# Two of the four channel groups of a causal depthwise convolution, moved from GpSimd and VectorE to TensorE as products with diagonal matrices

## Chip, cores and metric

One core of one Trainium2 chip runs the whole kernel in one launch. The metric is the device time in microseconds (us) of one execution. A measurement gives the median of several runs; a profile is one further execution, with its own time.

## The reference, cut to what matters

The kernel computes one decoder layer on 256 tokens of width 1024: a token mixer, cross-attention and a mixture of 32 experts. The mixer projects its input once and feeds three branches, a sparse attention (NSA), a convolution module and a gated linear attention (GLA), which are then merged. Only the convolution changes. It has 512 channels, 31 taps and is causal:

```python
a, gate = jnp.split(u_pair, 2, axis=-1)
u = a * jax.nn.sigmoid(gate)                      # (256 tokens, 512 channels)
y = conv(u, w, padding 30 on the left)            # y[t, c] = sum_k w[k, c] * u[t + k - 30, c], depthwise
y = y + b
out_b = silu(layer_norm(y, g, beta))              # over the 512 channels
```

## The kernel before, in words

**Layout.** Channels lie on the 128 partitions, in four groups m = 0 to 3 of 128 channels, and tokens along the free dimension. The tile `cu` (in the code `u`) holds the gated input with 30 zero columns in front, `cp` holds 34 numbers for each channel (31 taps, the bias, the norm's scale and shift), and `cy` (`y`) is the running sum.

**The taps.** `conv_out` (L305) returns the function `end`, which the layer calls at L601. It issues 31 taps for each of the four groups (L323 to L325). Groups 0, 1 and 2 go to VectorE (DVE): a `tensor_scalar` for tap 0 (L315), then 30 fused multiply-adds (L320). Group 3 goes to GpSimd (POOL), with two instructions for a tap: a product into one half of the tile `csg` (L317), then a sum (L318). So VectorE has 93 instructions and GpSimd 61.

**After the taps** come the layer norm over channels (L326 to L345), the gate (L346 to L348), and a split of the result into a high and a low part, `coh` and `col` (L349 to L351), which `merge` for branch 1 (L1611) multiplies by its weights.

**Splits.** Nearly every large product on TensorE is made from two fp32r halves of each operand. `wslot` (L121) gets 1 MB of weights by DMA; ScalarE (ACT) copies the high half `wh` (L80) and VectorE subtracts it to make the low half `wl` (L142, or L87 in four parts). Two such pairs are in flight. `project` (L145) then issues three matmuls for each block (L172). So every megabyte of weights passes through ACT and DVE before TensorE (PE) can use it.

**The order of the work.** A scheduler orders each engine's queue when the kernel is compiled: of what it takes to be ready it puts first what has the highest priority, and that is the order of the program, but for the blocks marked `high_priority`. At run time each engine works through its queue in that fixed order. `conv_out`'s `end` stands behind `gla` (L1596) and `nsa_in` (L1599) and ahead of `nsa` (L1607, which has high priority) and the three merges (L1610 to L1615). So taps fill places between the splits, the GLA and NSA inputs.

**GLA** (L426) is a chain over nine levels: differences and products on VectorE (L454 to L466), an exponential on ScalarE (L464), small matmuls on TensorE (L474 to L483) into banks of a pool of four PSUM banks (`bank`, L93), and copies on VectorE (L489 to L499). Then follow a norm with a power on GpSimd (L230), products (L518) and transposes (L91).

**After the front** (all up to about 430 us) the experts run: their weights, some 1 MB in each DMA, stream in on SyncE's queue while the matmuls of L1210 and L1255 use them.

Of the kernel before, what the change touches and what calls it, by code (L numbers as in the profile page):

```python
# [23 lines left out]
F32 = mybir.dt.float32  # L24
# [3 lines left out]
AF = mybir.ActivationFunctionType  # L28
ALU = mybir.AluOpType
# [5 lines left out]
P = 128  # L35
S = 256
# [5 lines left out]
TAPS = 31  # L42
# [28 lines left out]
class Front:  # L71
# [233 lines left out]
    def conv_out(self, pool):  # L305

        nc = self.nc
        u, cp = self.cu, self.cp
        y = pool.tile([P, 4, S], F32, name="cy")
        products = pool.tile([P, 4, S], F32, name="csg")  # L310
        def tap(m, k, v):
            scale, shift = cp[:, m, k:k + 1], cp[:, m, TAPS:TAPS + 1]
            eng = nc.gpsimd if m == 3 else nc.vector
            if k == 0:
                eng.tensor_scalar(y[:, m, :], u[:, m, 0:S], scale, shift, op0=ALU.mult, op1=ALU.add)  # L315
            elif m == 3:
                eng.tensor_scalar_mul(v, u[:, m, k:k + S], scale)  # L317
                eng.tensor_tensor(out=y[:, m, :], in0=y[:, m, :], in1=v, op=ALU.add)  # L318
            else:
                eng.scalar_tensor_tensor(y[:, m, :], u[:, m, k:k + S], scale, y[:, m, :], op0=ALU.mult, op1=ALU.add)  # L320

        def end():
            for k in range(TAPS):  # L323
                for m in range(4):
                    tap(m, k, products[:, k % 2, :])  # L325
            omean = pool.tile([P, P], F32, name="omean")  # L326
            nc.vector.memset(omean[:], 1.0 / 512)
            b = self.bank()
            for m in range(4):
                nc.tensor.matmul(b[:, 0:S], omean[:], y[:, m, :], start=(m == 0), stop=(m == 3))  # L330
            nc.vector.tensor_sub(y[:], y[:], b[:, None, 0:S].to_broadcast([P, 4, S]))
            sq = pool.tile([P, 4, S], F32, name="csg")
            nc.scalar.activation(sq[:], y[:], AF.Square)
            b = self.bank()
            for t in range(2):
                for m in range(4):
                    nc.tensor.matmul(b[:, t:t + 1], sq[:, m, t * P:t * P + P], omean[:, 0:1], start=(m == 0), stop=(m == 3))
            rs = pool.tile([P, 2], F32, name="crs")
            self.rpow(pool, rs[:], b[:, 0:2], 1e-5, 2)
            b = self.bank()  # L340
            for t in range(2):
                nc.tensor.matmul(b[:, t * P:t * P + P], rs[:, t:t + 1].to_broadcast([P, P]), self.ident[:], start=True, stop=True)
            nc.vector.tensor_mul(y[:], y[:], b[:, None, 0:S].to_broadcast([P, 4, S]))
            for m in range(4):
                nc.scalar.activation(y[:, m, :], y[:, m, :], AF.Identity, scale=cp[:, m, 32:33], bias=cp[:, m, 33:34])  # L345
            sg = pool.tile([P, 4, S], F32, name="csg")  # L346
            self.gate(sg[:], y[:])
            self.gated(y[:], sg[:], y[:])  # L348
            h = pool.tile([P, 4, S], F32R, name="coh", tag="cu")  # L349
            l = pool.tile([P, 4, S], F32R, name="col", tag="csg")  # L350
            self.split(h[:], l[:], y[:], 0.5)  # L351
            return h, l

        return end
# [1408 lines left out]
```

## Time and profile before

| what | value |
|---|---|
| median of 3 runs | 1439.58 us (1435.54 to 1441.28) |
| the profiled execution's own time | 1441.21 us |
| its span, first to last instruction | 1439.3 us |
| mean granted TensorE clock | 0.928 |
| busy over the span: PE / DVE / ACT / POOL | 85% / 42% / 24% / 9% |
| bytes moved by DMA | 472.24 MB, mean 328 GB/s |

Busy time is the time in which at least one instruction of the engine ran. Matmuls are pipelined, so a record's duration is longer than the distance to the next record; the distance between starts in an unbroken row of equal records is what one of them costs. PEld is the loading of the stationary operand, which runs beside the matmuls. An fp32 matmul shows as two records.

### The profile page before, as it was taken

The numbers are of one execution on the slowest core, as the hardware profiler recorded it, in microseconds if no ns is written. First come the engines' busy times: TensorE is split into PE (matmuls) and PEld (weight loads), VectorE is DVE, ScalarE is ACT, GpSimd is POOL, SyncE is SP. The second block draws the span as 40 slices with busy tenths as digits, with TensorE's granted clock in tenths as the row PEclk, the third lists the DMA queues.
The fourth block names the chain that finished last, engine by engine and source line by source line (L and its number), as shares of the span: only waits on it lengthen the run. The fifth ranks groups of instructions, "written<-read, shape, count | busy, mean of one in ns | idle before, by whom it ended". The sixth has DMA issues, their size and how long they took to land. (4 is left out here: it accounts for less than half of the span.)

```text
span 1439.3 us, 20736 instructions
## 1 busy us (share of the span) xinstructions
PE 1216.4 (85%) x8274; PEld 606.7 (42%) x8274; DVE 601.2 (42%) x1319; ACT 352.3 (24%) x711; POOL 136.6 (9%) x137
## 2 busy tenths in 40 slices
PE   8978999999999877886788978887987787898684
PEld 8767978989873211221222223122322121223121
DVE  5999876585643311332223223232332232323113
ACT  4424365444522110111111111121111021212100
POOL 3994000010011000030000000000000000000001
PEclk9989999999998987999999999899999998899888
DMA  9535816565878899999999879999999999869994
GB/s 305 174 74 125 241 60 189 180 212 179 312 286 314 357 415 415 414 416 416 417 414 415 346 299 413 415 370 413 416 415 413 415 416 416 351 273 414 416 416 177
DMA packets 110696, 472.24 MB, mean 328 GB/s; under 512 B 12081, under 2 KB 16276, under 8 KB 77756
## 3 DMA queue, kind: packets, MB, share of 16 engines
q1 hardware_dynamic: 108604, 464.63, 82.4%
q0 software_dynamic: 1648, 4.25, 1.3%
q8 instruction: 110, 1.80, 0.5%
q10 hardware_dynamic: 272, 1.05, 0.2%
q14 instruction: 62, 0.51, 0.1%
HBM read 468.58 MB, written 1.31 MB: 326 GB/s over the span
## 5 line engine op out<-in xcount | busy, mean ns | idle before, releaser
L1210 PE MATMUL g<-w,xT 128*32 128x512 f32 x1984 | 272.7, 659 | 84.7 <-DMA w<-in_expert_w_gu_dram 83.2
L1255 PE MATMUL m<-w,hT 128*32 128x512 f32 (+1 forms) x1440 | 206.0, 640 | 17.2 <-DMA w<-in_expert_w_down_dram 8.9
L1181 DVE TENSOR_SCALAR gc<-g 64x256 f32<-64x256 f32 (+1 forms) x70 | 29.2, 417 | 351.7 <-PE g L1210 251.1
L1210 PEld LDWEIGHTS g<-w,xT 128*32 128x32 f32 x1984 | 57.6, 114 | 270.5 <-DMA w<-in_expert_w_gu_dram 140.8
L142 DVE TENSOR_TENSOR wl<-w,wh 128x1024 fp32r<-128x1024 f32 (+1 forms) x96 | 114.9, 1233 | 65.8 <-ACT wh L80 65.6
L1182 ACT ACTIVATE row<-gc 64x256 f32<-64x256 f32 (+1 forms) x90 | 37.4, 417 | 383.5 <-DVE gc L1181 383.5
L80 ACT ACTIVATE wh<-w 128x1024 fp32r<-128x1024 f32 (+1 forms) x112 | 105.7, 990 | 102.0 <-PE big L172 66.6
L1229 DVE TENSOR_TENSOR ye<-ye,m 32x512 f32<-32x512 f32 x82 | 55.8, 681 | 143.6 <-ACT ye L80 142.4
L172 PE MATMUL big<-xh,wh 128*128 128x256 f32 x352 | 101.8, 289 | 0.0
L172 PE MATMUL big<-xl,wh 128*128 128x256 f32 x352 | 101.5, 288 | 0.0
L172 PE MATMUL big<-xh,wl 128*128 128x256 f32 x352 | 101.2, 288 | 0.0
L1255 PEld LDWEIGHTS m<-w,hT 128*32 128x32 f32 (+1 forms) x1440 | 47.1, 116 | 122.6 <-issue 95.1
L80 ACT ACTIVATE ye<-m 32x512 f32<-32x512 f32 (+1 forms) x83 | 48.8, 588 | 165.8 <-PE m L1255 164.8
L230 POOL TENSOR_TENSOR mv<-rp,nhalf 128x1 f32<-128x1 f32 x4 | 2.2, 554 | 893.6 <-DVE rp L229 800.9
L1210 PE MATMUL u<-w,xT 128*32 128x512 f32 x640 | 74.9, 609 | 0.0
L1266 PE MATMUL y<-ye,pgT 128*128 128x512 f32 x128 | 63.4, 641 | 9.8 <-issue 8.3
L172 PEld LDWEIGHTS big<-xl,wh 128*128 128x128 f32 x352 | 68.9, 196 | 1.1 <-issue 0.8
L172 PEld LDWEIGHTS big<-xh,wh 128*128 128x128 f32 x352 | 69.1, 196 | 0.2
L172 PEld LDWEIGHTS big<-xh,wl 128*128 128x128 f32 x352 | 68.5, 195 | 1.2 <-issue 1.1
L91 PE MATMUL m<-ident,uc 64*128 64x64 f32 (+1 forms) x168 | 29.1, 255 | 39.9 <-ACT hT L80 18.3
L1082 DVE TENSOR_SCALAR xT<-m,rowc 128x128 f32<-128x128 f32 x64 | 22.0, 405 | 84.4 <-PE m L91 73.4
L320 DVE SCALAR_TENSOR_TENSOR cy<-cu,cp,cy 128x256 f32<-128x256 f32 x90 | 48.2, 589 | 0.1
(431 smaller groups left out, 1767.5 us busy)
## 6 DMA issues: line engine op xcount, KB each, us to landing
w<-in_expert_w_gu_dram SPq DMA_DIRECT2D x256, 1024.0 KB
w<-in_expert_w_down_dram SPq DMA_DIRECT2D x127, 1024.0 KB
w<-in_w_in_dram SPq DMA_DIRECT2D x23, 1024.0 KB
w<-in_xa_wkv_dram SPq DMA_DIRECT2D x8, 1024.0 KB
w<-in_w_branch_dram SPq DMA_DIRECT2D x4, 1024.0 KB
w<-in_w_out_dram SPq DMA_DIRECT2D x4, 1024.0 KB
w<-in_xa_wq_dram SPq DMA_DIRECT2D x4, 1024.0 KB
w<-in_xa_wo_dram SPq DMA_DIRECT2D x4, 1024.0 KB
```

Of the source, the lines that this page charges most:

```text
L80: self.nc.scalar.activation(out, in_, AF.Copy, scale=scale)
L91: self.nc.tensor.transpose(out, in_, self.ident[0:k, 0:k])
L142: eng.tensor_tensor(out=l[:, js, :n], in0=t[:, js, :n], in1=h[:, js, :n].bitcast(F32), op=ALU.subtract)
L172: self.last = nc.tensor.matmul(dst, l, r, start=(b not in seen), stop=(last and i == 2), skip_group_check=True)
L320: eng.scalar_tensor_tensor(y[:, m, :], u[:, m, k:k + S], scale, y[:, m, :], op0=ALU.mult, op1=ALU.add)
L1082: self.nc.vector.tensor_scalar(out, in_, g, t, op0=ALU.mult, op1=ALU.add)
L1181: nc.vector.tensor_scalar_min(gc[0:n, s], g[:, s], 7.0)
L1182: nc.scalar.activation(sg[0:n, s], gc[0:n, s], AF.Sigmoid, scale=1.702)
L1210: nc.tensor.matmul(gu[32 * c:32 * c + 32, :], xT[:, k, :], W[k][:, c * 512:c * 512 + 512], start=(k == 0), stop=(k == 7), skip_group_check ...
L1229: nc.vector.tensor_add(ye[:, c, :], ye[:, c, :], pd[64 * c:64 * c + 32, :])
L1255: self.nc.tensor.matmul(pd[p0:p0 + w, :], hT[:, j, h * w:h * w + w], W[8 + k][:, c * 512:c * 512 + 512], start=(i < P // (2 * w)), stop=(i ...
L1266: self.nc.tensor.matmul(self.y[t][c][:], pgT[rows, t, :], ye[rows, v, :], start=False, stop=last, skip_group_check=True)
```

## The change

Groups 0 and 1 stay on VectorE as they were. Groups 2 and 3 become products on TensorE: for each tap k and group m ScalarE makes a 128x128 diagonal matrix whose diagonal holds the taps of the 128 channels (the identity times the column `cp[:, m, k]`), and TensorE multiplies it by the 256 shifted columns of `u` and adds into one half of a PSUM bank. These are plain fp32 products. The eight diagonals in flight lie in the space of `csg`. The bank, one of the pool of four, is held from the first product to the end. Two ScalarE instructions then copy its halves to `y` and add the bias. GpSimd does none of the convolution any more. No DMA is added, removed or moved.

```diff
         y = pool.tile([P, 4, S], F32, name="cy")
-        products = pool.tile([P, 4, S], F32, name="csg")
-        def tap(m, k, v):
+        diag = pool.tile([P, 4, S], F32, name="csg")[:].rearrange("p m (h c) -> p (m h) c", h=2)
+        mine = (2, 3)
+
+        def tap(m, k):
             scale, shift = cp[:, m, k:k + 1], cp[:, m, TAPS:TAPS + 1]
-            eng = nc.gpsimd if m == 3 else nc.vector
             if k == 0:
-                eng.tensor_scalar(y[:, m, :], u[:, m, 0:S], scale, shift, op0=ALU.mult, op1=ALU.add)
-            elif m == 3:
-                eng.tensor_scalar_mul(v, u[:, m, k:k + S], scale)
-                eng.tensor_tensor(out=y[:, m, :], in0=y[:, m, :], in1=v, op=ALU.add)
+                nc.vector.tensor_scalar(y[:, m, :], u[:, m, 0:S], scale, shift, op0=ALU.mult, op1=ALU.add)
             else:
-                eng.scalar_tensor_tensor(y[:, m, :], u[:, m, k:k + S], scale, y[:, m, :], op0=ALU.mult, op1=ALU.add)
+                nc.vector.scalar_tensor_tensor(y[:, m, :], u[:, m, k:k + S], scale, y[:, m, :], op0=ALU.mult, op1=ALU.add)
+
+        def product(bank, m, k, i):
+
+            d = diag[:, i % 8, :]
+            nc.scalar.activation(d, self.ident[:], AF.Identity, scale=cp[:, m, k:k + 1])
+            nc.tensor.matmul(bank, d, u[:, m, k:k + S], start=(i == 0), stop=(k == TAPS - 1), skip_group_check=True)

         def end():
+            b = self.bank()
             for k in range(TAPS):
                 for m in range(4):
-                    tap(m, k, products[:, k % 2, :])
+                    if m in mine:
+                        i = mine.index(m)
+                        product(b[:, i * S:i * S + S], m, k, k * len(mine) + i)
+                    else:
+                        tap(m, k)
+            for i, m in enumerate(mine):
+                nc.scalar.activation(y[:, m, :], b[:, i * S:i * S + S], AF.Identity, bias=cp[:, m, TAPS:TAPS + 1])
```

## Rows read from the trace of the kernel before

**Rows 1.** The page: the span, and from the part with 40 equal slices (36 us each) the busy tenths of PE and DVE, the granted TensorE clock in tenths, and the DMA rate in GB/s.

```profile
span 1439.3 us, 20736 instructions
...
PE   8978999999999877886788978887987787898684
...
DVE  5999876585643311332223223232332232323113
...
PEclk9989999999998987999999999899999998899888
...
GB/s 305 174 74 125 241 60 189 180 212 179 312 286 314 357 415 415 414 416 416 417 414 415 346 299 413 415 370 413 416 415 413 415 416 416 351 273 414 416 416 177
```

**Rows 2.** Busy time of each engine in three stretches (us from the span's start). Columns: length of the stretch; busy us and number of instructions of PE, PEld, DVE, ACT, POOL; granted clock; DMA share; GB/s.

```profile
36.00:152.00 116.00, 98.13 (x883) 88.69 (x883) 110.89 (x205) 44.26 (x77) 84.97 (x76) 0.93 0.51 127
152.00:420.00 268.00, 267.81 (x1812) 239.11 (x1811) 174.99 (x268) 128.44 (x248) 8.86 (x14) 1.00 0.60 203
420.00:1439.30 1019.30, 818.72 (x5352) 248.17 (x5351) 297.07 (x819) 162.77 (x363) 31.23 (x22) 0.91 0.95 385
```

**Rows 3.** TensorE's groups of matmuls by line and shape between 36 and 152 us. Columns: names, shapes, count | busy us, mean ns of one | idle us of the engine before them and what ended it. Of the first, second and fourth form there are three groups each, with the operands' halves exchanged (xl,wh and xh,wl; wh,xh and wh,xl), and of the L396 form too (xl,mh and xh,ml).

```profile
L172 PE MATMUL big<-xh,wh 128*128 128x256 f32 x118 | 35.0, 296 | 0.0
...
L172 PE MATMUL big<-wl,xh 128*128 128x512 f32 x32 | 13.6, 424 | 4.8 <-DVE wl L142 4.8
...
L483 PE MATMUL s<-gx 64*64 64x64 f32 x192 | 6.6, 231 | 6.5 <-DVE gad L495 5.4 <-DVE gx L466 1.1
...
L172 PE MATMUL big<-wl,xh 128*128 128x256 f32 x16 | 4.6, 289 | 0.2 <-DVE wl L142 0.2
...
L508 PE MATMUL s<-gv,gat 128*128 128x128 f32 x16 | 3.5, 346 | 0.0
...
L396 PE MATMUL s<-xh,mh 128*56 128x256 f32 x8 | 2.3, 282 | 0.0
...
L91 PE MATMUL s<-ident,goc 128*128 128x128 f32 x8 | 1.8, 288 | 3.1 <-DVE goc L518 3.1
...
L477 PE MATMUL s<-gx 64*64 64x64 f32 x16 | 0.9, 222 | 2.6 <-DVE gx L466 2.6
```

**Rows 4.** The timeline of TensorE (start us, duration us, instruction): the first and the last of 17 consecutive 256-column records, and the first and the last of 12 consecutive 512-column records.

```profile
102.00 0.28 PE L172 MATMUL big<-xl,wh 128*128 128x256 f32 x1
...
103.92 0.28 PE L172 MATMUL big<-xh,wl 128*128 128x256 f32 x1
...
53.35 0.39 PE L172 MATMUL big<-wl,xh 128*128 128x512 f32 x1
...
55.85 0.39 PE L172 MATMUL big<-wh,xh 128*128 128x512 f32 x1
```

**Rows 5.** Busy time in ten microseconds of the later front (columns as in Rows 2).

```profile
300.00:310.00 10.00, 10.00 (x46) 8.29 (x45) 7.28 (x11) 3.01 (x4) 1.00 (x1) 1.00 0.61 208
```

**Rows 6.** VectorE: the page's group of the taps (count | busy us, mean ns); then the taps and the weight split between 36 and 107 us (same columns); then the line views of the taps and of the split over the whole run (ns min/median/max, first and last start us).

```profile
L320 DVE SCALAR_TENSOR_TENSOR cy<-cu,cp,cy 128x256 f32<-128x256 f32 x90 | 48.2, 589 | 0.1
...
L320 DVE SCALAR_TENSOR_TENSOR cy<-cu,cp,cy 128x256 f32<-128x256 f32 x34 | 21.2, 678 | 0.0
...
L142 DVE TENSOR_TENSOR wl<-w,wh 128x1024 fp32r<-128x1024 f32 x11 | 15.0, 1399 | 0.0
...
L320 DVE SCALAR_TENSOR_TENSOR cy<-cu,cp,cy x90: 462/481/2547, 43.2 to 161.6; 128x256 f32<-128x256 f32 x90
...
L142 DVE TENSOR_TENSOR wl<-w,wh x96: 693/1221/1761, 16.0 to 405.7; 128x1024 fp32r<-128x1024 f32 x94, 128x512 fp32r<-128x512 f32 x2
```

**Rows 7.** GpSimd's two groups of conv instructions between 36 and 107 us (count | busy us, mean ns | idle before).

```profile
L317 POOL TENSOR_SCALAR csg<-cu,cp 128x256 f32<-128x256 f32 x30 | 42.5, 1427 | 16.9 <-DVE cp L288 16.8
...
L318 POOL TENSOR_TENSOR cy<-cy,csg 128x256 f32<-128x256 f32 x30 | 26.9, 896 | 1.3
```

**Rows 8.** The line views of two products of fp32 by fp32, 128x128 by 128x256 (two records each; of the first also its weight loads; ns min/median/max, first and last start us).

```profile
L763 PEld LDWEIGHTS s<-xkT,xq x32: 186/190/192, 359.3 to 366.1; 128*128 128x128 f32 x32
...
L763 PE MATMUL s<-xkT,xq x32: 377/379/483, 359.4 to 366.3; 128*128 128x256 f32 x32
...
L330 PE MATMUL s<-cy,omean x8: 379/379/483, 161.3 to 163.0; 128*128 128x256 f32 x8
```

**Rows 9.** ScalarE between 0 and 440 us: a 128x128 activation with a per-partition operand, and a copy of 128x256 out of PSUM (count | busy us, mean ns | idle before).

```profile
L615 ACT ACTIVATE ns<-ns,nmx 128x128 f32<-128x128 f32 x16 | 6.2, 393 | 3.3 <-DVE nmx L610 3.3
...
L80 ACT ACTIVATE gax<-s 128x256 f32<-128x256 f32 x2 | 0.7, 382 | 6.0 <-PE s L474 6.0
```

**Rows 10.** Busy time in four stretches of 4 us (columns as in Rows 2).

```profile
76.00:80.00 4.00, 4.00 (x16) 3.15 (x16) 4.00 (x8) 0.00 (x0) 3.92 (x5) 0.81 0.49 131
88.00:92.00 4.00, 3.89 (x29) 3.77 (x30) 4.00 (x7) 0.00 (x0) 3.92 (x4) 0.50 0.35 57
92.00:96.00 4.00, 4.00 (x36) 3.80 (x35) 4.00 (x8) 0.00 (x0) 3.92 (x5) 0.68 0.59 171
112.00:116.00 4.00, 4.00 (x26) 3.69 (x25) 3.88 (x11) 1.28 (x6) 0.00 (x0) 0.62 0.59 225
```

**Rows 11.** The tile col, the conv branch's result: when it is made and when TensorE first loads its weights with coh and col (ns min/median/max, first and last start us).

```profile
L85 DVE SCALAR_TENSOR_TENSOR col<-cy,coh x1: 1217/1217/1217, 210.1 to 210.1; 128x1024 fp32r<-128x1024 f32 x1
...
L172 PEld LDWEIGHTS big<-col,wh x32: 187/188/192, 228.5 to 253.2; 128*128 128x128 f32 x32
```

**Rows 12.** The waits between 36 and 152 us (us in total, times, longest us).

```profile
ACT gd L464 <- DVE gd L463: 12.2, 5, 4.2
```

## The prediction

> **What bounds the kernel now.** I read the page's slices first, then busy time by stage, then each engine inside the stage that the change touches.
>
> The slices show two regimes [rows 1]. From about slice 13 the DMA rate stands near 415 GB/s: the experts are paced by their weights, a fixed number of bytes (DMA share 0.95 from 420 us on [rows 2]). What the front loses or gains therefore reaches the end one for one, unless something re-orders the experts, which nothing here does. So the question is how long the front takes.
>
> The front has two parts [rows 2]. From 36 to 152 us VectorE is busy 110.9 of 116 us, TensorE 98.1, GpSimd 85.0, ScalarE 44.3. From 152 to 420 us TensorE is busy 267.8 of 268 us. There its records stand shoulder to shoulder: 46 in ten microseconds are 0.217 us each [rows 5], and an unbroken row of 512-column records runs at (55.85 - 53.35)/11 = 0.227 us [rows 4]. So TensorE sets the pace from 152 us on, and VectorE before that. All the convolution's taps lie in or close to the first part, the last one at 161.6 us [rows 6]. The branch's result `col` is there at 210.1 us and first used at 228.5 us [rows 11]: the convolution itself has 18 us to spare. The change matters only through what it does to the queues of others.
>
> How much of the 116 us does TensorE need? The 256-column records number 3x118 + 3x16 + 3x8 = 426 [rows 3] at (103.92 - 102.00)/16 = 0.120 us [rows 4], 51.1 us. The 512-column ones are 96 at 0.227, 21.8 us. The other 361 records are short; the four groups of them shown (232 records, 12.8 us busy [rows 3]) give 20 us for all in proportion, too much, since the busy time of a burst holds its tail. The weight loads, 88.7 us [rows 2], leave 15.8 for them. So TensorE needs 89 to 93 us and has 23 to 27 us of slack; I take 27, nearer to the loads because of the tails.
>
> That slack divides so. Waits for VectorE's low halves: 4.8 + 0.2 = 5.0 us; for the GLA copies `gad`, 5.4; for `gx`, 1.1 + 2.6 = 3.7; for `goc`, 3.1 [rows 3]. Time lost to the granted clock, busy time times what is missing from 1.00 (below 1 the stretch was partly at 1.2 GHz instead of 2.4): 4.00x0.19 + 3.89x0.50 + 4.00x0.32 + 4.00x0.38 = 5.5 us [rows 10], all right behind such waits. That leaves 4.3 us in small pieces.
>
> **What the change takes away.** VectorE loses 31 of its 93 tap instructions. 90 took 48.2 us [rows 6], 0.536 each, so 16.6 us. GpSimd loses all 61, 42.5 + 26.9 us and one more [rows 7]. While GpSimd worked, the taps took 678 ns on average against a median of 481, and the split 1399 against 1221 [rows 6]. If the remaining two thirds of the 34 taps fall to the median, 23x0.197 = 4.5 us return, and from 11 splits 2.0 us. VectorE would then stand at 110.9 - 16.6 - 6.5 = 88 of 116 us: no longer the bound.
>
> **What it adds.** 62 fp32 products of 128x128 by 128x256. The kernel has the same form elsewhere: 32 records over 359.4 to 366.3 us are 0.2226 each [rows 8], two for a product, 0.445 us. So 62x0.445 = **27.6 us of TensorE**. The other row of the form, 8 records in 161.3 to 163.0, gives 0.486 and 30.1 us as the upper end; its times are rounded over a seventh of the length, so I take the first.
>
> ScalarE makes 62 diagonals. No row has this exact instruction; a 128x128 activation with a per-partition operand took 393 ns, a whole 128x256 copy out of PSUM 382 [rows 9]. So 24.4 us for the diagonals and 0.8 for the two copies at the end, on an engine with 71.7 us free in the stretch. I cost them at nothing: idle ScalarE hides them. If that cover fails, a diagonal ahead of a weight copy makes it late by 0.4 us, and the low half and the three matmuls behind it too. The reverse wait is the risk: with eight diagonals in flight (3.6 us of products), TensorE stands when ScalarE is held longer. The PSUM bank held throughout leaves three for GLA. Fewer banks can't speed anything; the worst is some of the GLA waits above again. I take nothing, and leave it to the third case. No DMA is added or moved; what SyncE and GpSimd issue stays in its queue, and GpSimd's comes free earlier.
>
> **The sum.** How much of the 27 us do the lighter VectorE and the products between them fill? The waits for low halves and `gad` (10.4 us) are VectorE's backlog: I take 8.4 back. The slow clock followed these holes: 5.0 of 5.5. The `gx` and `goc` waits (6.8) are a chain through three engines in which products can stand, if the compiled order puts them there: half, 3.4. Of the small pieces half, 2.1. Together 18.9 us. These four shares are my estimates; the ends are 7 (only part of the backlog) and 27. So the front grows by 27.6 - 18.9 = **8.7 us**. Against the profiled execution's own 1441.2 us that is 1449.9; that execution stood 1.6 above the median of the runs, so against 1439.6 it is **1448 us**. The reasoning in a line: VectorE's backlog costs TensorE less than the work handed to it.
>
> Which measure of TensorE's room counts is the point on which a rule of the skill bears: busy matmul time leaves 116 - 98.1 = 17.9 us, the count of records 23 to 27 [rows 2, 4]. The Trainium skill (Perfetto Trace Analysis, Identifying the Most-Contended Engine) says that matmul busy time is no good measure of headroom, that the busy share of weight loading is better, and that the engine with the highest occupancy should be relieved first. By busy matmul time the change would cost at least 27.6 - 17.9 = 9.7 us; by the rule VectorE is the engine to relieve and the change should not hurt. The trace agrees with the rule on the measure from 36 to 152 us, and not after it, where weight loading is 8.29 of 10 us and the records leave no room [rows 5].
>
> **Rivals.**
>
> *Every hole is filled (not slower).* VectorE at 88 of 116 us is late for nothing, the products stand in every hole of GLA, and TensorE runs at full clock from 36 to 152 us. Then all 27 us come back: 27.6 - 27 = +0.6, 1440 us. If TensorE were held by its weight loads alone, a product would cost two loads of 190 ns [rows 8], 62x0.38 = 23.6, and the time would be 27 - 23.6 = 3.4 below, 1436 us. For it: the need for the products and the slack are of one size. Against it: TensorE's queue is fixed, and a chain of three engines keeps holes. It decides once less than about 6 us of holes are left.
>
> *Coupled queues (much slower).* A product waits for its diagonal, a diagonal for the product eight before it, and both stand in queues with the splits and GLA. ScalarE already stood 12.2 us in five waits for VectorE's `gd`, the longest 4.2 us [rows 12], longer than eight products last. If TensorE inherits these, only about 7 us come back: 27.6 - 7 = +20.6, 1460 us. Against it: the lighter VectorE shortens just these waits.
>
> *The products don't go into the holes.* They stand behind GLA and NSA inputs in priority, and share a pool of banks with them. If they come in one block after about 147 us, where TensorE is full, only the backlog and the clock come back, 13.4 us: +14.2, 1454 us. Against it: taps in the same place of the program began at 43.2 us [rows 6].
>
> **How the numbers follow.** A measurement of this kernel tells about 0.5%, 7.2 us, from no change: the lines are 1432.4 and 1446.8 us. The forecast, +4 to +13 us, has 0.56, of which 0.37 is above the upper line and 0.19 within. Every hole filled has 0.22: 0.17 within, and 0.05 faster, for what a re-ordered front may gain besides. Coupled queues have 0.15 and one block 0.07, both slower. So slower 0.59, same 0.36, faster 0.05. The range 1437 to 1460 reaches into the filled case and to the middle of the coupled one, and leaves out some 0.15; it holds the upper price of a product (+2.5 us).
>
> **What the changed profile should show.** No taps on GpSimd, 60 on VectorE with a mean near 490 ns. 124 product records at about 0.222 us apart where they are unbroken. VectorE between 36 and 152 us near 75% busy. The granted clock near 1.00 through the holes of before. Waits of TensorE for low halves and `gad` under 3 us. The stretch that did the work of 36 to 152 us longer by about 9 us, and the same work after it unchanged. `col` before it is needed. I am wrong if TensorE's stretch is not longer (all filled), if TensorE waits for diagonals by more than 5 us (coupled), or if the front's growth does not reach the end of the run.

## The result, and the profile after

The changed kernel takes **1455.55 us** (median of 6 runs, 1453.01 to 1458.59) against 1440.95 (6 runs) before: a ratio of 1.0092, 95% interval 1.0071 to 1.0113, or +13.3 us (the two medians differ by 14.6). The prediction was 1448 in 1437 to 1460, slower at 0.59. The profiled execution after took 1456.01 us, span 1454.2. Of one kernel below, the one with only VectorE's group as products, two of six runs (1474.29 and 1476.88 us) were in a slower state of the chip and are left out.

First the same three stretches as in [rows 2].

```profile
36.00:152.00 116.00, 109.43 (x951) 99.15 (x950) 88.81 (x192) 63.58 (x129) 15.83 (x15) 0.99 0.57 156
152.00:420.00 268.00, 266.43 (x1790) 239.08 (x1789) 161.81 (x238) 130.08 (x254) 8.68 (x12) 0.97 0.50 169
420.00:1454.00 1034.00, 831.83 (x5442) 265.88 (x5440) 305.58 (x833) 167.46 (x369) 31.83 (x23) 0.92 0.95 385
```

VectorE (the third busy time) fell from 110.9 to 88.8 us and the clock of the first stretch rose from 0.93 to 0.99: the relief is real. But the second stretch, at 1.00 before, is now at 0.97.

VectorE between 36 and 107 us, answering to [rows 6] (count | busy us, mean ns):

```profile
L318 DVE SCALAR_TENSOR_TENSOR cy<-cu,cp,cy 128x256 f32<-128x256 f32 x44 | 18.5, 480 | 0.0
L142 DVE TENSOR_TENSOR wl<-w,wh 128x1024 fp32r<-128x1024 f32 x12 | 16.4, 1400 | 0.0
L87 DVE TENSOR_TENSOR wl<-w,wh 128x512 fp32r<-128x512 f32 x8 | 5.0, 690 | 0.0
```

The small split before, in the same view:

```profile
L87 DVE TENSOR_TENSOR wl<-w,wh 128x512 fp32r<-128x512 f32 x8 | 7.0, 934 | 0.0
```

The taps dropped from 678 to 480 ns; the small split L87 from 934 to 690. The large split did not (1399 before; the reason is in the last section).

TensorE's groups between 36 and 165 us, with the idle time before them, answering to [rows 3]:

```profile
L324 PE MATMUL s<-cu,csg 128*128 128x256 f32 x124 | 27.0, 379 | 0.0
L172 PE MATMUL big<-wl,xh 128*128 128x512 f32 x32 | 12.5, 390 | 0.0
...
L494 PE MATMUL s<-gx 64*64 64x64 f32 x192 | 5.9, 224 | 1.2 <-DVE gad L506 0.8 <-DVE gx L477 0.4
...
L91 PE MATMUL s<-ident,goc 128*128 128x128 f32 x8 | 2.1, 338 | 4.0 <-DVE goc L529 4.0
...
L488 PE MATMUL s<-gx 64*64 64x64 f32 x16 | 0.9, 222 | 1.1 <-DVE gx L477 1.1
```

The waits for low halves are gone (5.0 before) and that for `gad` is 0.8 (5.4 before). The wait for `goc` is still there, at 4.0: no product stands in it. Where the products stand is in the tile view of the diagonals (first and last start at the end of the times) and in the timeline of TensorE (start, duration):

```profile
L324 PE MATMUL s<-cu,csg x124: 377/379/484, 131.7 to 158.4; 128*128 128x256 f32 x124
L323 ACT ACTIVATE csg<-ident,cp x62: 387/401/404, 38.4 to 155.3; 128x128 f32<-128x128 f32 x62
```
```profile
131.37 0.39 PE L589 MATMUL s<-cw,cmy 64*15 64x64 f32 x4
131.69 1.56 PE L324 MATMUL s<-cu,csg 128*128 128x256 f32 x6
...
157.28 1.46 PE L324 MATMUL s<-cu,csg 128*128 128x256 f32 x6
158.57 0.38 PE L341 MATMUL s<-cy,omean 128*128 128x256 f32 x1
```

All 124 records stand in **one block of 27 us**, right behind the last matmul of the NSA inputs (L589) and right ahead of the convolution's own mean (L341). While it runs VectorE waits 28.4 us for that mean. Behind it TensorE is slow. The 16 us from 160 to 176 before, then the same stretch after, then the wait in the latter:

```profile
160.00:176.00 16.00, 16.00 (x135) 15.51 (x134) 10.92 (x18) 5.07 (x5) 0.71 (x1) 1.00 0.64 227
```
```profile
160.00:176.00 16.00, 14.61 (x92) 13.99 (x91) 8.84 (x18) 6.63 (x20) 1.64 (x1) 0.68 0.18 67
```
```profile
166.78 0.80 PE L353 MATMUL s<-ident,crs 128*128 128x128 f32 x2 [1.39 <-POOL crs L230]
```

The convolution's norm is a chain from engine to engine with short matmuls, and after the block less other work stands beside it: in these 16 us 92 matmuls for 135, and between the mean (L341) and the chain's matmuls with `crs` (L353) 25 records of L172 where before there were 53. TensorE is idle for 1.4 us, and the granted clock goes from 1.00 to 0.68, partly at 1.2 GHz instead of 2.4. It is 1.00 up to 165.4 us, where the wait begins, and 0.53 in the wait and 0.50 in the 5.2 us behind it. So 1.4 + 14.6 x 0.32 = 6.1 us are lost here, an estimate that takes the clock's whole loss as time.

Milestones, taken in every kernel from the line views of three tiles: the last matmuls of the NSA inputs, the first product of `xkT` with `xq`, and the first expert matmul (start, us).

```
                 NSA inputs end   first xq   first expert   span
before               148.3          359.4        435.5      1439.3
after                131.1          378.9        454.6      1454.2
```

The work up to the NSA inputs ends 17.2 us earlier, the block puts 27 on top (its end, 158.6, is 9.7 after the 148.9 of before), and by the first expert matmul the delay is 19.1 us, so another 9.4 came behind the block. Not all of that is loss. The windows up to the end of the NSA inputs (before, then after), and one later stretch after:

```profile
0.00:148.85 148.85, 126.75 (x1088) 116.23 (x1088) 126.14 (x227) 59.10 (x99) 96.51 (x102) 0.93 0.59 170
```
```profile
0.00:131.55 131.55, 119.91 (x1076) 111.63 (x1076) 105.35 (x216) 61.31 (x107) 27.21 (x41) 0.96 0.64 190
220.00:260.00 40.00, 39.95 (x304) 37.38 (x304) 23.18 (x28) 18.59 (x31) 2.79 (x6) 0.96 0.67 198
```

TensorE did 1088 matmuls up to there before and 1076 after: 12 records of L172, at 0.12 us 1.4 us, only moved behind this milestone. With the 6.1 us of the norm's chain and 0.04 x 40 = 1.6 us of clock between 220 and 260 us that is 9.1 of the 9.4. `col` is made at 201.5 us and first used at 249.9: it is not late.

### The profile page after: what moved, and what is told of

It is laid out like the page before. It is cut to its first block, busy times and chain, and to the rows that moved or that the text cites. A ratio compares the mean times of both kernels' runs of the same rounds, so it can differ in the third digit from the quotient of the medians.

```text
span 1454.2 us, 20956 instructions
## 1 busy us (share of the span) xinstructions
PE 1238.6 (85%) x8398; PEld 634.5 (44%) x8398; DVE 573.1 (39%) x1288; ACT 377.0 (26%) x775; POOL 67.7 (5%) x76
## 5 line engine op out<-in xcount | busy, mean ns | idle before, releaser
L1266 PE MATMUL m<-w,hT 128*32 128x512 f32 (+1 forms) x1440 | 202.7, 635 | 18.6 <-DMA w<-in_expert_w_down_dram 10.3
L172 PE MATMUL big<-xh,wh 128*128 128x256 f32 x352 | 103.6, 294 | 0.0
L172 PE MATMUL big<-xl,wh 128*128 128x256 f32 x352 | 103.0, 293 | 0.0
L172 PE MATMUL big<-xh,wl 128*128 128x256 f32 x352 | 102.7, 293 | 0.0
L80 ACT ACTIVATE ye<-m 32x512 f32<-32x512 f32 (+1 forms) x83 | 48.8, 588 | 158.6 <-PE m L1266 157.6
L172 PEld LDWEIGHTS big<-xl,wh 128*128 128x128 f32 x352 | 70.4, 200 | 1.7 <-issue 1.6
L172 PEld LDWEIGHTS big<-xh,wh 128*128 128x128 f32 x352 | 70.6, 201 | 0.3
L172 PEld LDWEIGHTS big<-xh,wl 128*128 128x128 f32 x352 | 70.1, 200 | 1.3 <-issue 1.1
L91 PEld LDWEIGHTS m<-ident,uc 64*128 64x128 f32 (+1 forms) x168 | 17.4, 144 | 70.1 <-ACT hT L80 29.9
L1277 PEld LDWEIGHTS y<-ye,pgT 128*128 128x128 f32 x128 | 24.4, 200 | 46.7 <-issue 46.4
```

Of the source, the lines that this page charges most:

```text
L80: self.nc.scalar.activation(out, in_, AF.Copy, scale=scale)
L91: self.nc.tensor.transpose(out, in_, self.ident[0:k, 0:k])
L172: self.last = nc.tensor.matmul(dst, l, r, start=(b not in seen), stop=(last and i == 2), skip_group_check=True)
L1266: self.nc.tensor.matmul(pd[p0:p0 + w, :], hT[:, j, h * w:h * w + w], W[8 + k][:, c * 512:c * 512 + 512], start=(i < P // (2 * w)), stop=(i ...
L1277: self.nc.tensor.matmul(self.y[t][c][:], pgT[rows, t, :], ye[rows, v, :], start=False, stop=last, skip_group_check=True)
```

## Experiments

Theory A: the place in the program decides; the products, written behind GLA and the NSA inputs, come out as a block and leave the holes unused. Rivals: the shared pool of banks holds them back; the diagonals on ScalarE do; or the kernel simply has no room for 27.6 us. Ratios are to the kernel before on the same chip (its medians there: 1440.73 for the first four kernels below, 1441.24 for the next four, 1441.99 for the last three).

**A bank of its own for the products**

```diff
-            b = self.bank()
+        acc = self.ps_c.tile([P, 512], F32, name="cacc")
...
-        f.ps_s = front.enter_context(tc.tile_pool(name="ps_s", bufs=4, space=PSUM, side="right"))
+        f.ps_s = front.enter_context(tc.tile_pool(name="ps_s", bufs=3, space=PSUM, side="right"))
+        f.ps_c = front.enter_context(tc.tile_pool(name="ps_c", bufs=1, space=PSUM, side="right"))
```

> The products' PSUM bank comes from a pool of its own (one bank; the shared pool keeps three) and is asked for ahead of GLA. Theory A, the place in the program decides (lowest priority of what waits for TensorE until the NSA inputs are done): most of the 62 products still run in one block of about 24 to 27 us right behind the NSA inputs, 1453 to 1458 us. Theory B, the products only waited for one of the four banks that GLA and the NSA inputs keep taking: they begin near 40 us, stand in the holes, and the time is 1440 to 1447 us.

1454.07 us, 1.0088 [1.0059, 1.0117]. The products still form a block, 4.6 us earlier:

```profile
L324 PE MATMUL cacc<-cu,csg x124: 376/379/484, 127.1 to 154.6; 128*128 128x256 f32 x124
```

The first of them now stand ahead of the last matmul of the NSA inputs (131.3 us), but none near 40 us. The bank theory falls.

**No products, no diagonals** (the relief alone)

```diff
-                    if m in mine:
-                        i = mine.index(m)
-                        product(b[:, i * S:i * S + S], m, k, k * len(mine) + i)
-                    else:
+                    if m not in mine:
                         tap(m, k)
...
-                nc.scalar.activation(y[:, m, :], b[:, i * S:i * S + S], AF.Identity, bias=cp[:, m, TAPS:TAPS + 1])
+                nc.scalar.activation(y[:, m, :], u[:, m, 0:S], AF.Identity, bias=cp[:, m, TAPS:TAPS + 1])
```

> The products and their diagonals are left out (groups 2 and 3 get only the first shifted columns plus bias), so VectorE and GpSimd are relieved and TensorE and ScalarE get nothing. If the relief is worth what the trace of the changed kernel shows at the end of the NSA inputs (131.2 against 148.3 us): 1420 to 1424 us without any further gain, down to 1415 if the slow stretch behind the block of products goes too. Rival, TensorE's later work sets the front's end whatever happens before 150 us: 1437 to 1441 us.

1434.99 us, 0.9965 [0.9949, 0.9981]. The total lies between the two expectations. The front is the theory's: the first expert matmul comes at 420.5 us, 15.0 before that of before. The rest went in the experts, which took 1013.1 us from there on, against 1003.8 before. The clock is 1.00 where the norm's chain runs, so the relief alone does not slow it. Since two channel groups are not the convolution's here, tokens go to other experts; a later experiment checks this.

**The identity in place of the diagonals**

```diff
-            d = diag[:, i % 8, :]
-            nc.scalar.activation(d, self.ident[:], AF.Identity, scale=cp[:, m, k:k + 1])
-            nc.tensor.matmul(bank, d, u[:, m, k:k + S], start=(i == 0), stop=(k == TAPS - 1), skip_group_check=True)
+            nc.tensor.matmul(bank, self.ident[:], u[:, m, k:k + S], start=(i == 0), stop=(k == TAPS - 1), skip_group_check=True)
```

> The 62 products stay, but all take the identity as their stationary operand and ScalarE makes no diagonals (the sums of groups 2 and 3 are then unweighted). Theory A, part of the loss is that the 54 diagonals of the block (23.3 us of ScalarE) hold back the weight copies, so that TensorE is short of work and slow behind the block from 164 to 176 us: the copies are made during the block, 1446 to 1450 us. Rival, the block itself costs everything: 1454 to 1457 us.

1482.53 us, 1.0301 [1.0269, 1.0333]. The front is that of the change to within 0.3 us (first xq 379.1, first expert matmul 454.9), block included:

```profile
L322 PE MATMUL s<-cu,ident x124: 376/379/483, 131.9 to 158.5; 128*128 128x256 f32 x124
```

So the diagonals cost the front nothing, and do not place the block. The longer total lies behind 454.9 us: the overflow group of the experts (tile `xTo`) has 256 records against 192, so it too has other tokens.

**The products spread ahead of GLA's levels** (bank asked for ahead of GLA)

```diff
+        acc = self.bank()
+        def feed():
+            for k in range(TAPS):
+                for i, m in enumerate(mine):
+                    product(acc[:, i * S:i * S + S], m, k, k * len(mine) + i)
+                    yield
+        self.feed = feed()
...
+            for _ in range(7):
+                next(self.feed, None)
```

> As the changed kernel, but seven products stand ahead of each of GLA's nine levels in the program, and the bank is asked for ahead of GLA. Theory A, the order cost the difference to the forecast: the products fill GLA's waits, the block behind the NSA inputs and the slow stretch behind it are gone, 1440 to 1448 us. Rival, coupled queues: TensorE waits for diagonals and ScalarE for products inside GLA, 1453 to 1465 us.

1444.86 us, 1.0019 [0.9998, 1.0041]; first expert matmul 441.6, 13.0 before that of the change. The products' records (tile view), and the two stretches:

```profile
L324 PE MATMUL s<-cu,csg x124: 376/379/484, 74.0 to 109.4; 128*128 128x256 f32 x124
```
```profile
36.00:152.00 116.00, 114.06 (x970) 101.65 (x969) 84.18 (x192) 66.32 (x139) 14.30 (x14) 1.00 0.48 129
152.00:420.00 268.00, 267.82 (x1822) 238.27 (x1822) 165.19 (x242) 128.12 (x245) 8.28 (x13) 1.00 0.58 198
```

TensorE's idle time in the first stretch is 1.9 us (6.6 in the change) and the clock is 1.00 in both: the holes are filled and the norm's chain has cover again (more other matmuls beside it). By the two ratios order alone is worth 0.0073, about 10 us of the 13.3. It does not turn the change into a gain.

**The block alone, on the kernel before** (62 products with the identity, their sum times zero added; no relief)

```diff
+            spare = self.bank()
+            for k in range(TAPS):
+                for i in range(2):
+                    nc.tensor.matmul(spare[:, i * S:i * S + S], self.ident[:], u[:, 2 + i, k:k + S], start=(k + i == 0), stop=(k == TAPS - 1), skip_group_check=True)
+            for i in range(2):
+                nc.vector.scalar_tensor_tensor(y[:, i, :], spare[:, i * S:i * S + S], 0.0, y[:, i, :], op0=ALU.mult, op1=ALU.add)
```

> The kernel before with 62 fp32 products of the identity added behind its taps (no diagonals, nothing taken from VectorE or GpSimd; the sum is added times zero), so TensorE gets the block and nobody is relieved. Theory A (a block of products costs its full 27 us in a place where TensorE is full, and the experts pass it on one for one): the first expert matmul comes 25 to 30 us later than before's 435.5, and the time is 1465 to 1471 us. Rival (the experts give back part of what the front loses, as 19.1 us of delay at the first expert matmul became 14.9 at the end of the changed kernel): the front is later by as much, and the time is 1458 to 1464 us.

1472.11 us, 1.0229 [1.0191, 1.0266]. The tile views of the products and of the experts' tokens `xT`:

```profile
L329 PE MATMUL s<-cu,ident x124: 377/379/483, 148.6 to 175.3; 128*128 128x256 f32 x124
```
```profile
L1216 PE MATMUL g<-w,xT x1984: 589/592/1062, 463.5 to 1402.6; 128*32 128x512 f32 x199
```

The first expert matmul is 28.0 us later, for 27.6 forecast as the price of the products; the span grows by 27.2, the median by 30.9, 1.1 us more than theory A's upper end. What the front loses does reach the end. Behind this block the norm's chain is not slow: the clock of the second stretch is 1.00 and the wait for `crs` 0.35 us, with 33 records of L172 between mean and `crs`.

```profile
152.00:420.00 268.00, 267.50 (x1820) 239.82 (x1819) 163.30 (x248) 122.89 (x238) 7.77 (x12) 1.00 0.52 174
```
```profile
184.51 0.49 PE L348 MATMUL s<-ident,crs 128*128 128x128 f32 x2 [0.35 <-POOL crs L230]
```

So neither the block alone nor the relief alone slows the chain; in the change, which has both, it is slow. Why it has only 25 records there stays open.

**The data of "no products" on the kernel before**

```diff
+            for m in (2, 3):
+                nc.scalar.activation(y[:, m, :], u[:, m, 0:S], AF.Identity, bias=cp[:, m, TAPS:TAPS + 1])
```

> The kernel before with all its taps, but groups 2 and 3 are then overwritten by what the kernel without products puts there, so that the experts get the same tokens as in that run. It is the base for the relief alone. Theory A (the relief is worth at the end what it is worth at the first expert matmul, 15 us, and the other tokens made that run's experts longer): 1446 to 1451 us. Rival (the experts give the front's 15 us back): 1439 to 1442 us, 5 us above the run without products.

1472.47 us, 1.0224 [1.0188, 1.026]. As a base for times it failed: the overwriting copies stand in ScalarE's queue until GpSimd's last tap, 28.5 us, TensorE waits 25.3 us for GLA's `gad` behind them, and the front ends 21.3 us late. What it does show: its expert part takes 1014.0 us, as in the kernel without products (1013.1). The other tokens explain the longer experts there.

**Only GpSimd's group as products** (VectorE keeps three groups, four products ahead of each level; the edit is against the spread kernel)

```diff
-        mine = (2, 3)
+        mine = (3,)
-            for _ in range(7):
+            for _ in range(4):
```

> Only GpSimd's group becomes 31 products, four ahead of each of GLA's levels; VectorE keeps three groups of taps. Theory A (GpSimd's work mattered because VectorE's instructions are longer beside it): VectorE gets some 6 us back in the splits and taps, the products cost 13.8 us of which GLA's waits hide about half: 1438 to 1444 us. Rival (VectorE's own taps are what holds TensorE): the relief is small and the time is 1446 to 1452 us.

**1435.47 us, 0.9962 [0.9945, 0.9978]**: faster than both kernels. The first stretch, and VectorE between 36 and 107 us:

```profile
36.00:152.00 116.00, 111.63 (x983) 99.37 (x982) 105.48 (x227) 57.30 (x110) 18.03 (x16) 1.00 0.53 154
```
```profile
L318 DVE SCALAR_TENSOR_TENSOR cy<-cu,cp,cy 128x256 f32<-128x256 f32 x56 | 23.6, 478 | 0.0
L142 DVE TENSOR_TENSOR wl<-w,wh 128x1024 fp32r<-128x1024 f32 x10 | 11.8, 1218 | 0.0
```

First xq comes at 355.8 us, 3.6 before that of before, but the first expert matmul at 435.2, only 0.3 before. Between them stands a wait of TensorE on its own sequencer, ahead of the first expert matmul (the first line is before, the second this kernel; us, times, longest):

```profile
PE g L1210 <- PEq L1407: 1.1, 1, 1.1
```
```profile
PE g L1231 <- PEq L1428: 4.2, 1, 4.2
```

It is 0.3 to 1.2 us in the other kernels, but for the next one (3.6), so there the milestone of the first expert matmul stands some 3 us late. What makes it long is not known.

**Only VectorE's group as products** (GpSimd keeps its own; four diagonals in flight; against the kernel with GpSimd's group)

```diff
-        mine = (3,)
+        mine = (2,)
+            eng = nc.gpsimd if m == 3 else nc.vector
...
-            d = diag[:, i % 8, :]
+            d = diag[:, i % 4, :]
```

> Only VectorE's third group becomes 31 products, four ahead of each of GLA's levels (four diagonals in flight); GpSimd keeps its group. Theory A (GpSimd's work lengthens VectorE's instructions): VectorE loses 16.6 us of taps but stays slowed: 1442 to 1449 us, above the run that moves GpSimd's group. Rival (VectorE's taps are the bound, GpSimd is harmless): 1434 to 1440 us, below it.

1456.44 us (median of 4 runs, 1452.25 to 1459.02), 1.01 [1.0066, 1.0135]: above the ranges of both theories, on theory A's side. VectorE's taps between 36 and 107 us, and TensorE's waits between 36 and 152 us (us, times, longest):

```profile
L325 DVE SCALAR_TENSOR_TENSOR cy<-cu,cp,cy 128x256 f32<-128x256 f32 x36 | 24.1, 724 | 0.0
```
```profile
PE s L511 <- DVE gad L523: 8.4, 1, 8.4
PE big L172 <- DVE wl L142: 7.0, 4, 2.6
```

As many products as in the kernel ahead of it, and VectorE with 31 taps fewer, yet 21.0 us slower: with GpSimd at work each tap takes 724 ns, not 478, and TensorE waits for VectorE as before the change. ScalarE also waited 16.7 us for products with only four diagonals in flight, so not all of the 21.0 is GpSimd's; how much stays open.

**Every tap on VectorE, nothing on GpSimd or TensorE** (against the kernel before)

```diff
-            eng = nc.gpsimd if m == 3 else nc.vector
+            eng = nc.vector
-            elif m == 3:
-                eng.tensor_scalar_mul(v, u[:, m, k:k + S], scale)
-                eng.tensor_tensor(out=y[:, m, :], in0=y[:, m, :], in1=v, op=ALU.add)
```

> All four channel groups stay taps and all of them run on VectorE (124 taps): no products, no diagonals, nothing of the convolution on GpSimd. Theory A (GpSimd's work beside VectorE lengthens VectorE's own instructions, and that, not the number of taps, is what held TensorE): taps near 480 ns on average, L142 near 1220 and L87 near 690 from 36 to 107 us; the 31 taps more cost 31 x 0.478 = 14.8 us of VectorE and the contention gives some 7 to 12 back, so VectorE is still the nearest engine to full, and the front ends within 5 us of before: first expert matmul 431 to 440 us, 1436 to 1446 us. Rival B (VectorE's count of instructions decides): the 15 us come straight onto the front, first expert matmul 446 to 452 us, 1450 to 1457 us.

1436.45 us, 0.9966 [0.9949, 0.9983]; first expert matmul 430.0. The two stretches, and the taps between 36 and 107 us:

```profile
36.00:152.00 116.00, 109.27 (x1025) 101.76 (x1024) 110.90 (x240) 51.19 (x85) 15.20 (x15) 0.99 0.64 179
152.00:420.00 268.00, 261.20 (x1810) 228.97 (x1809) 173.67 (x276) 123.92 (x243) 11.65 (x16) 0.98 0.55 184
```
```profile
L317 DVE SCALAR_TENSOR_TENSOR cy<-cu,cp,cy 128x256 f32<-128x256 f32 x45 | 21.1, 532 | 0.0
```

VectorE is busy for the same 110.9 us as before, but its 240 instructions there are 35 more, and TensorE does 1025 in place of 883. A tap takes 532 ns on average, 678 before; theory A had asked for some 480. So simply taking GpSimd's help away is a gain. Its limit shows in the second stretch: the last tap starts at 166.1 us, and TensorE is idle for 6.8 us and at 0.98.

**GpSimd's group as products, in the change's own place** (against the change)

```diff
-        mine = (2, 3)
+        mine = (3,)
```

> As the kernel with GpSimd's group alone as products (31 of them, VectorE keeps its three groups), but the products are written where the change has them, behind GLA and NSA inputs, not ahead of GLA's levels. Theory A (place in the program decides): the 62 records stand in one block of 13 to 14 us after 125 us, TensorE's idle time from 36 to 152 us is not used, and the first expert matmul comes 5 to 9 us after that of the spread kernel (435.2): 440 to 444 us, 1441 to 1446 us. Rival B (13.8 us of products are too few for their place to matter, the rest of the front moves up into the same holes): first expert matmul 434 to 438 us, 1434 to 1439 us.

1441.04 us, 0.9993 [0.9979, 1.0007]; first xq 361.1, first expert matmul 437.5. Again a block (133.9 to 147.2 us), with the holes left (109.10 us busy of 116, clock 0.97). Against the kernel with the same products spread it is 5.3 us later at xq, 2.3 at the first expert matmul, and 0.0031 by the ratios, 4.5 us. The first and the last speak for theory A. The other spoke for the rival only because the spread kernel's long wait stands in it: TensorE's wait ahead of the first expert matmul is 1.2 us here and 4.2 there, and without the 3.0 the difference is 5.3 again. So the place of 13.8 us of products is worth some 5 us.

**Half of GpSimd's group as products** (16 taps, two ahead of each level; the other 15 on VectorE; against the kernel with GpSimd's whole group, spread)

```diff
+HALF = 16
-            nc.tensor.matmul(bank, d, u[:, m, k:k + S], start=(i == 0), stop=(k == TAPS - 1), skip_group_check=True)
+            nc.tensor.matmul(bank, d, u[:, m, k:k + S], start=(i == 0), stop=(k == HALF - 1), skip_group_check=True)
-            for k in range(TAPS):
+            for k in range(HALF):
+                for k in range(HALF, TAPS):
+                    tap(m, k)
-            for _ in range(4):
+            for _ in range(2):
```

> As the kernel with GpSimd's group alone as products, spread ahead of GLA's levels, but only 16 of its 31 taps are products (two ahead of each level); the other 15 are taps on VectorE, and GpSimd has none. Theory A (TensorE is the engine that still lacks room in the front once GpSimd is quiet): 15 products fewer, 6.7 us of TensorE, 15 taps more on VectorE, 7.2 us, which it has; first expert matmul 430 to 434 us, 1431 to 1435 us. Rival B (VectorE is as full as TensorE again): the gain is used up, first expert matmul 434 to 439 us, 1435 to 1441 us.

**1426.29 us (1423.02 to 1428.13, 6 runs), 0.9896 [0.9877, 0.9915]**, the fastest of all; first xq 351.1, first expert matmul 426.1. Theory A's direction, and further than it went. The two stretches, and the tile view of `xT`:

```profile
36.00:152.00 116.00, 109.59 (x1001) 100.10 (x1001) 111.41 (x242) 53.29 (x98) 18.24 (x15) 1.00 0.63 168
152.00:420.00 268.00, 264.49 (x1872) 232.35 (x1870) 170.21 (x271) 130.21 (x250) 14.21 (x18) 1.00 0.57 195
```
```profile
L1234 PE MATMUL g<-w,xT x1984: 589/592/1063, 426.1 to 1360.4; 128*32 128x512 f32 x199
```

The front is 9.4 us shorter: 15.0 of relief less 16 x 0.445 = 7.1 of products would be 7.9, if VectorE's 46 taps more than in the kernel without products cost nothing. The span is 16.2 shorter, so 6.8 us come from the expert part, which no edit touches. There (first expert matmul to the end) it takes 997.0 us; the other kernels that route the same tokens took 999.6 to 1003.9. TensorE's waits for weights there are 74.2 us against 83.2 before, but in the slower kernel with the whole group they are 73.1, so this does not explain it. It stays open.

## Why the prediction was right, and where its working was not

The kernel is slower by 13.3 us where 8.7 was forecast, inside the range. The size came closest to the third rival, one block (+14.2, given 0.07), and the mechanism is that rival's. That the time lies inside the range is in part luck: terms that the working had wrong cancel, as shown below.

- **VectorE's relief: right.** 88.8 us busy for 88 forecast; taps at 480 for 490. Waits for low halves and `gad` came to 0.8 where under 3 was asked. The relief by itself is 15.0 us at the first expert matmul (the kernel without products), for 8.4 + 5.0 = 13.4 forecast from backlog and clock.
- **The price of the products: right.** 27.0 us for 124 records; 28.0 at the first expert matmul in the block alone, for 27.6.
- **Diagonals at nothing: right in the front.** Without them it is the same to 0.3 us. Among TensorE's waits none is for a diagonal, so the coupled queues did not come. The bank at nothing: also right, a bank of its own changes nothing.
- **Products in the holes: wrong.** This is the step of the working that failed. I gave half of `gx`, `goc` and the small pieces (3.4 + 2.1 us) to products "if the compiled order puts them there", and used the fact that the taps began at 43.2 us against the block. That row was of another engine: the taps moved up in VectorE's queue, the products stayed behind GLA and the NSA inputs in TensorE's until they were written between GLA's levels. The spread kernel fills 4.6 us more of the holes (6.6 idle to 1.9), near the 5.5 that I had counted.
- **"The same work after it unchanged": wrong, and I had no term for it.** Of the 9.4 us that came behind the block 1.4 is work that only moved there; the rest is loss, most of it in the norm's chain, where TensorE waited and the clock fell. Before, the same 16 us ran at clock 1.00, and the second stretch does so again in the spread kernel. That the chain was slow for lack of other matmuls beside it is inferred from the counts of records (53 before, 33 behind the block alone, 25 in the change); no run changes that number by itself. In the kernel without products 2.3 us go the same way (17.3 us early at the NSA inputs' end, 15.0 at the experts), and there too 12 records, 1.4 us, only moved. The stretch up to the block's end was 9.7 us longer, by chance near the 8.7 forecast.
- **One for one to the end: right within a few us.** 28.0 gives 27.2 (span) or 30.9 (medians) in the block alone. Of the change's 19.1 at the first expert matmul the span shows 14.9: its expert part took 999.6 us against 1003.8, a spread that other kernels with the same tokens show as well. The rival's +14.2 came close by terms that cancel: +9.4 behind the block against -3.8 of more relief (17.2 at the NSA inputs' end for 13.4; the 1.4 of moved work stands in both), -0.6 for the block (27.0 for 27.6), -4.2 in the experts and -1.6 from span to medians.

The account at the first expert matmul, from kernels that each have one part: relief -15.0 (no products), products +28.0 (block alone), together +13.0; the change has +19.1. The 6.1 left is what the two parts cost only together, and is of the size of the loss in the 16 us behind the block. The spread kernel stands at +6.1, below the +13.0 of the parts: 4.6 of holes filled, and 0.01 x 116 = 1.2 of clock in the first stretch; some 1 us is not accounted for.

The rule that I weighed (the Trainium skill, Perfetto Trace Analysis, Identifying the Most-Contended Engine: relieve the engine with the highest occupancy) named VectorE, and the traces agree: relief alone is 15.0 us. They do not bear out that the change could then not hurt. What decided was where the work went and, more than the number of VectorE's instructions, who worked beside it: removing GpSimd's part alone gave 5.5 us (medians, and at the first expert matmul) with 31 more taps on VectorE, while 62 taps fewer from there (430.0 to 420.5 at the first expert matmul) gave 9.5, or 4.8 for a group of 31.

## What to carry to other kernels

A row that shows one engine starting early says nothing of where another engine's new work will stand: look at what is ahead of it in that engine's queue, and feed it between the waits by hand if it is to fill holes. A block on the bounding engine costs itself, and can cost the work behind it too when that is left as a bare chain: here it did with VectorE relieved and did not without, so price that chain too. Before moving work off a busy VectorE, ask what its instructions cost without GpSimd beside them; here moving GpSimd's group alone beat moving both, and half of it beat that.

## What the runs showed of the hardware that was not expected

An instruction of VectorE can be held for nearly the whole of a GpSimd instruction. In the change GpSimd only does a few splits, and this is one (timelines, start and duration), with one in the kernel with GpSimd's group as products:

```profile
103.66 2.43 POOL L142 TENSOR_TENSOR wl<-w,wh 128x1024 fp32r<-128x1024 f32 x1 [1.89 <-PE s L91]
...
103.79 3.38 DVE L142 TENSOR_TENSOR wl<-w,wh 128x1024 fp32r<-128x1024 f32 x1
```
```profile
118.45 2.97 POOL L142 TENSOR_TENSOR wl<-w,wh 128x1024 fp32r<-128x1024 f32 x1 [2.68 <-ACT wh L80]
...
119.15 2.55 DVE L318 SCALAR_TENSOR_TENSOR cy<-cu,cp,cy 128x256 f32<-128x256 f32 x1
```

The split took 3.38 us for a median of 1.22: it began 0.13 us after GpSimd's and ended 1.1 after it. The tap took 2.55 for 0.48 and ended 0.3 after GpSimd's. The one split of 3.38 among twelve is why their mean stayed at 1400 ns: (3.38 - 1.22)/12 = 0.18. The Trainium skill (SBUF — State Buffer, SBUF: two separate sides) says that the two engines share a pair of ports that one of them holds for its whole instruction, and that a VectorE instruction with two SBUF inputs meets it; the two rows agree in that both VectorE instructions end only after GpSimd's has ended, though what is left of the tap then, 0.3 us, is less than its usual 0.48 (the spans of GpSimd are rough). I had priced this as an average of 0.2 us a tap.
